# A transformer layer on one core: the last block product of an output projection made of seven smaller ones

## The chip, the cores and the metric

The kernel runs on one core of one Trainium2 chip. The time is the device time of one execution in microseconds; the number that counts is the median of the timed runs. The core has five engines: the PE (TensorE, matmuls; its weight loads are listed apart as PEld), DVE (VectorE), ACT (ScalarE), POOL (GpSimd), and SP (SyncE), which here only issues DMAs.

## The reference, cut to what matters

512 tokens, 2048 features, all in float32.

```
h = rmsnorm(x, norm_g)
y = attention(h)                      # 32 query heads, 4 key heads, window of 128, gated by silu
x = x + y @ w_out                     # "out projection", 512 x 2048 by 2048 x 2048
g = sigmoid(rmsnorm(x, ple_norm) @ ple_gate)
x = x + (p @ ple_proj) * g            # "gate stage"
return rmsnorm(x, final_g)
```

## The kernel before, in words

A product in float32 is made of three matmuls in a reduced format (`mm3`, lines 124 to 126): each operand is split into a high part (a cast by ACT) and a low part (operand minus high part, by DVE), and high x high, high x low and low x high are summed in PSUM.

The out projection and the gate stage each take a 512 x 2048 by 2048 x 2048 product as two by two blocks, made of seven block products instead of eight (Strassen's scheme in Winograd's form). The order of the seven is `ORDER_OUT = (1, 7, 2, 6, 5, 3, 4)`. Each product takes one sum of token blocks (a "form", made by `Forms.steps`, L734 to L747, in place in the tiles `gate`) and one sum of weight blocks. The sums of weights of products 7, 5 and 6 are made early, in DRAM, by copies and accumulating DMAs (`sum_weights`). Products 6 and 4 share one chain: the weights of product 6 are loaded into eight tiles `grown`, and as soon as they are split an accumulating DMA of POOL's queue adds another block to them for product 4 (L628).

Each product has two column halves (`jj`) and four pieces each. A piece is 256 rows by 512 columns of weights, 1024 columns in the tile; twelve matmuls of 512 columns use it. So the out projection has 56 pieces. `Pieces` (L613 on) looks after them: `_prepare` loads a piece into `braw` (three buffers) by a DMA of SP's queue, `_split` casts it into `bhi` (ACT, L641) and subtracts into `blo` (DVE, L642; three buffers each), and `ahead(i)` splits up to piece i + 2 and loads up to piece i + 3 when piece i is used.

Results are added to the residual tiles `x1` by `add_y` (DVE, L955 and L957), and `squares` (ACT, L924) sums their squares. `turn` transposes finished rows of `x1` (four transposes of 128 x 128 on the PE, L938) and writes them, times a gain, into `hT` (ACT, L941). These turns stand beside product 4 and the first product of the gate stage, whose forms (`fhg`, `flg`) come from `hT`.

In this part of the kernel only the PE and SP keep the written order. A scheduler places the instructions of DVE, ACT and POOL, and the program's data order then ties the engines by semaphores.

Of the kernel before, what the change touches and what calls it, by code (L numbers as in the profile page):

```python
# [11 lines left out]
F32 = mybir.dt.float32  # L12
# [43 lines left out]
def trunk_kernel(ctx: ExitStack, tc: tile.TileContext, a: dict):  # L56
# [557 lines left out]
    class Pieces:  # L614
# [2 lines left out]

        def __init__(self):
            self.specs, self.base, self.made, self.grown, self.due = [], {}, {}, {}, []

        def add(self, kind, srcs, key=None):
            self.specs.append((kind, srcs, key))
# [12 lines left out]
            self.base[i] = t  # L635

        def _split(self, i):
            raw = self.base.pop(i)
            hi = wpool.tile([P, WE], F32R, tag="whi", name=f"bhi{i}")
            lo = wpool.tile([P, WE], F32R, tag="wlo", name=f"blo{i}")  # L640
            nc.scalar.copy(hi, raw)  # L641
            nc.vector.tensor_sub(lo, raw, hi.bitcast(F32))  # L642
# [12 lines left out]
        def ahead(self, i):  # L655

            last = len(self.specs) - 9
            for n in range(max(i, 0), min(i + 6, last) + 1):
                kind = self.specs[n][0]
                if n not in self.base and n >= self.done and kind != "grow" and (kind == "seed" or n <= i + 3):  # L660
                    self._prepare(n)
            while self.done <= min(i + 2, last):
                self._split(self.done)
                self.done += 1

        def get(self, i):
            self.ahead(i)

            key = self.specs[i][2]
            if key is not None:  # L670
                n = next((n for n in range(i + 1, len(self.specs)) if self.specs[n][2] == key), None)
                if n is not None:
                    self.due.append((i + 6, n))
            while self.due and self.due[0][0] <= i:
                self._prepare(self.due.pop(0)[1])
            return self.made.pop(i)

    B = Pieces()

    def add_stage(nm, order):  # L680
        at = {}

        def add_embeds(p, jj):
            if nm == "ple_gate" and p in (1, 5, 3, 4):
                j = jj + 2 * (p in (5, 3))
                B.add("proj", a["ple_proj"].rearrange("(k p) d -> p k d", p=P)[:, :, j * 512 : (j + 1) * 512])

        for p in order:
            for jj in range(2):
                if nm == "ple_gate" and (p, jj) == (4, 0):  # L690
                    for v in range(2):
                        at["e", v] = len(B.specs)
                        add_embeds(p, v)
                at[p, jj] = len(B.specs)
                for m in range(4):
# [4 lines left out]
                    growing = (6, 4) if (nm, 6) in SUMS else (7, 6, 4)  # L700
# [6 lines left out]
    at_out = add_stage("w_out", ORDER_OUT)  # L707
    at_ple = add_stage("ple_gate", ORDER_PLE)

    class Forms:  # L710
# [6 lines left out]
        def steps(self, p):  # L717

            self.made[p] = []
            for h in range(2):  # L720
                a11, a21 = self.q[h][:, :, :256], self.q[h][:, :, 256:]
                a12, a22 = self.q[2 + h][:, :, :256], self.q[2 + h][:, :, 256:]
                if self.nm == "o":
                    src, sub = {
                        1: (a11, None), 7: (a11, (a21, a11)), 2: (a12, None), 6: (a11, (a22, a11)),
                        5: (a21, (a21, a22)), 3: (a12, (a12, a11)), 4: (a22, None),
                    }[p]
                else:
                    src, sub = {
                        2: (a12, None), 7: (a21, (a21, a11)), 1: (a11, None), 6: (a21, (a22, a21)),  # L730
                        5: (a11, (a11, a21)), 3: (a12, (a12, a21)), 4: (a22, None),
                    }[p]
                if sub:
                    nc.vector.tensor_sub(src, *sub)  # L734
# [135 lines left out]

    late = pool("late", reuse_waits="tile")
    rooms.append(late)
    x1 = [late.tile([P, NB, 512], F32, name=f"x1_{j}") for j in range(4)]
    fg = late.tile([P, D], F32, name="fg")
    pTh = late.tile([P, 2, S], F32R, name="pTh")
# [6 lines left out]
    def banks(p, jj, nm):  # L882

        if p in (6, 5, 3):
            return chain[jj]
        tag = ("to" if p in (7, 2) else "sp")[jj]
# [38 lines left out]

    hT = {}

    def turn(kp, th, tag):

        g = kp // 2  # L930
        if g not in hT:
            hT[g] = quarter(f"hT{g}")
        tp = bank(f"tp{kp}_{th}", tag)
        for n in range(2):
            k = 2 * kp + n
            for tb in range(2):
                src = x1[k // 4][:, 2 * th + tb, (k % 4) * P : (k % 4 + 1) * P]
                nc.tensor.transpose(tp[:, (2 * n + tb) * P : (2 * n + tb + 1) * P], src, ident)  # L938
        for n in range(2):
            k = 2 * kp + n  # L940
            nc.scalar.mul(hT[g][:, k % 4, th * 256 : th * 256 + 256], tp[:, n * 256 : n * 256 + 256], pn[:, k : k + 1])  # L941

    ple_forms = Forms(hT, "g")
    ple_first = ple_forms.steps(2)
# [15 lines left out]

    turns = []

    x_at = {(1, 1, 1): 0, (7, 0, 0): 2, (7, 0, 3): 1, (7, 1, 1): 3}
    waiting = {(7, 0): (1, 0), (2, 0): (1, 1)}
    held = {}
    for n, p in enumerate(ORDER_OUT):
        nxt = out_forms.steps(ORDER_OUT[n + 1]) if n < 6 else iter(())
        for jj in range(2):
            later.extend(held.pop(waiting.get((p, jj)), ()))
            calls = iter(range(4))  # L970

            def todo():
                part = x_at.get((p, jj, next(calls)))
                if part is not None:
                    load_x(part)
                next(nxt, None)
                if p == 4:
                    for tag in "to":
                        if turns:
                            turn(*turns.pop(0), tag)  # L980
                    if jj:
                        next(ple_first, None)

            ps = unit(p, jj, at_out, out_forms, todo)
            posts = [partial_of(add_y, p, jj, tb, ps[tb]) for tb in range(2)]
            if p == 1:
                held[p, jj] = posts
            else:
                later.extend(posts)
        run(nxt)  # L990
        if p == 6:
            nc.sync.dma_start(fg, a["final_g"].partition_broadcast(P))
        if p == 3:
            turns = [(kp, 0) for kp in range(8)] + [(kp, 1) for kp in range(4, 8)]
    run(ple_first)
    assert not turns

# [72 lines left out]

    spare = late.tile([P, 2 * WE], F32R, name="spare")
# [12 lines left out]
    for n, p in enumerate(ORDER_PLE[:-1]):  # L1086
        nxt = ple_forms.steps(ORDER_PLE[n + 1])
        for jj in range(2):
            calls = iter(range(4))

            def todo():
                k = early.get((p, jj, next(calls)))
                if turns:
                    turn(*turns.pop(0), "s")
# [184 lines left out]
```

## Time and profile before

| | before |
|---|---|
| median of 3 runs | 799.96 us (799.6 to 800.24) |
| the profiled execution | 798.73 us, span 797.0 us, granted clock 0.997 |
| PE busy | 785.5 us, 99% |
| DVE busy | 590.5 us, 74% |
| ACT busy | 482.7 us, 61% |
| POOL busy | 149.6 us, 19% |
| out projection on the PE | 452.52 to 610.28 us, 56 pieces |

All times inside the profile count from the start of its span. The span is what the profiler saw from the first to the last instruction; the execution's own time has a little around it. Busy matmul time is modelled and counts overlapping matmuls, so the distance between the starts of two matmuls says what one costs.

### The profile page before, as it was taken

To read this page: it belongs to the slowest core of one execution; us is meant where nothing else is said; L and a number is where in the kernel's file an instruction comes from. 1 tells how busy PE (TensorE), PEld (TensorE's weight loads), DVE (VectorE), ACT (ScalarE), POOL (GpSimd) and SP (SyncE) were. 2 spreads that over 40 slices of the span, in tenths; PEclk is the share of its full clock that TensorE was granted. 3 is DMA by queue.
4 is the path that set the end of the run, shared out by engine and by line. 5 is a ranking of instruction groups with operands and counts; after the bars stand their busy time and mean duration, and the time that the engine had idled before them with its cause. 6 is when DMAs were issued, how large, how long until landed. Compare 5 with 4: busy or idle time off the path is not lost.

```text
span 797.0 us, 11130 instructions
## 1 busy us (share of the span) xinstructions
PE 785.5 (99%) x3760; PEld 656.1 (82%) x3760; DVE 590.5 (74%) x1013; ACT 482.7 (61%) x992; POOL 149.6 (19%) x363
## 2 busy tenths in 40 slices
PE   9999999999999999999999999999999999999995
PEld 7888888888888888888888888888888888878884
DVE  4436478888877787787887898766656977979686
ACT  5632377677556766566665654555568756758545
POOL 0003013443243314332133200030000020200000
PEclk9999999999999999999999999999999999999998
DMA  8790586889687967879585578998503996885533
GB/s 336 279 212 11 187 237 180 235 211 260 175 226 193 220 199 211 213 207 260 155 220 135 151 267 312 353 258 249 197 26 118 358 208 211 163 212 194 176 106 106
DMA packets 44073, 163.99 MB, mean 206 GB/s; under 512 B 6304, under 2 KB 6944, under 8 KB 40176
## 3 DMA queue, kind: packets, MB, share of 16 engines
q1 hardware_dynamic: 36896, 129.01, 48.1%
q0 software_dynamic: 6832, 33.88, 23.0%
q8 instruction: 29, 0.48, 0.2%
q10 hardware_dynamic: 288, 0.39, 0.1%
q14 instruction: 28, 0.23, 0.1%
HBM read 157.44 MB, written 46.19 MB: 255 GB/s over the span
## 4 chain that ended last, share of the span: by engine, by line
PE 85%; issue 7%; DMA 3%; DVE 3%; POOL 1%; ACT 1%; SPq 0%; DVEq 0%; POOLq 0%; ACTq 0%
PE qps L126 7%; PE qps L124 7%; PE qps L125 7%; PE gps L124 7%; PE gps L125 7%; PE gps L126 7%; PE o L124 6%; PE o L126 6%; PE o L125 6%; PE s L401 2%; PE g L125 2%; PE g L126 2%; PE g L124 2%; PE o L523 2%; PE vps L228 2%
## 5 line engine op out<-in xcount | busy, mean ns | idle before, releaser
L642 DVE TENSOR_TENSOR blo<-braw,bhi 128x1024 fp32r<-128x1024 f32 x80 | 97.7, 1223 | 40.4 <-ACT bhi L641 40.2
L641 ACT CAST bhi<-braw 128x1024 fp32r<-128x1024 f32 x80 | 84.0, 1051 | 56.3 <-PE o L126 16.4
L124 PE MATMUL gps<-xh,whi 128*128 128x512 f32 x256 | 100.5, 393 | 0.0
L125 PE MATMUL gps<-xl,whi 128*128 128x512 f32 x256 | 100.0, 391 | 0.0
L126 PE MATMUL gps<-xh,wlo 128*128 128x512 f32 x256 | 99.9, 390 | 0.0
L503 POOL TENSOR_SCALAR_AFFINE_SELECT own<-r 64x256 fp32r<-64x256 f32 x96 | 61.2, 637 | 193.0 <-ACT r L484 109.3
L113 DVE TENSOR_TENSOR wlo<-wraw,whi 128x1024 fp32r<-128x1024 f32 x60 | 73.5, 1226 | 25.8 <-ACT whi L107 24.3
L124 PE MATMUL qps<-xh,whi 128*128 128x512 f32 x224 | 87.7, 392 | 0.0
L124 PE MATMUL o<-bhi,fho 128*128 128x512 f32 x224 | 87.7, 391 | 0.0
L125 PE MATMUL qps<-xl,whi 128*128 128x512 f32 x224 | 87.4, 390 | 0.0
L126 PE MATMUL qps<-xh,wlo 128*128 128x512 f32 x224 | 87.3, 390 | 0.0
L126 PE MATMUL o<-bhi,flo 128*128 128x512 f32 x224 | 87.2, 389 | 0.0
L125 PE MATMUL o<-blo,fho 128*128 128x512 f32 x224 | 87.2, 389 | 0.0
L461 ACT ACTIVATE t<-t,sm 128x129 f32<-128x129 f32 x128 | 50.6, 397 | 49.3 <-DVE sm L452 46.5
L125 PE MATMUL g<-blo,fhg 128*128 128x512 f32 x192 | 74.8, 390 | 0.4 <-DVE blo L642 0.4
L124 PE MATMUL g<-bhi,fhg 128*128 128x512 f32 x192 | 75.1, 391 | 0.0
L126 PE MATMUL g<-bhi,flg 128*128 128x512 f32 x192 | 74.8, 390 | 0.0
L107 ACT CAST whi<-wraw 128x1024 fp32r<-128x1024 f32 x60 | 62.1, 1037 | 16.1 <-DMA wraw<-in_w_q 16.1
L484 ACT CAST r<-pt 128x256 fp32r<-128x256 f32 x64 | 23.8, 372 | 55.4 <-PE pt L479 55.1
L126 PEld LDWEIGHTS gps<-xh,wlo 128*128 128x128 f32 x256 | 48.1, 188 | 10.6
L124 PEld LDWEIGHTS gps<-xh,whi 128*128 128x128 f32 x256 | 48.1, 188 | 9.1
L125 PEld LDWEIGHTS gps<-xl,whi 128*128 128x128 f32 x256 | 48.1, 188 | 8.7
(204 smaller groups left out, 1699.4 us busy)
## 6 DMA issues: line engine op xcount, KB each, us to landing
wraw<-in_w_gate_in SPq DMA_DIRECT2D x32, 512.0 KB, 5.4
wraw<-in_w_q SPq DMA_DIRECT2D x28, 512.0 KB, 6.2
w_out<-in_w_out POOLq DMA_DIRECT2D x24, 512.0 KB, 7.8
braw<-in_w_out SPq DMA_DIRECT2D x24, 512.0 KB, 4.0
braw<-in_ple_gate SPq DMA_DIRECT2D x24, 512.0 KB, 4.3
w_out<-in_w_out SPq DMA_DIRECT2D x16, 512.0 KB, 7.6
ple_gate<-in_ple_gate SPq DMA_DIRECT2D x16, 512.0 KB, 6.5
ple_gate<-in_ple_gate POOLq DMA_DIRECT2D x16, 512.0 KB, 6.1
```

The source lines that it names most:

```text
L107: nc.scalar.copy(hi, self.raw[i])
L113: nc.vector.tensor_sub(lo, raw, hi.bitcast(F32))
L124: nc.tensor.matmul(ps, sh, mh, start=first, stop=False, skip_group_check=more)
L125: nc.tensor.matmul(ps, sh, ml, start=False, stop=False, skip_group_check=more)
L126: nc.tensor.matmul(ps, sl, mh, start=False, stop=last, skip_group_check=more)
L228: nc.tensor.matmul(v_ps[t], h[:, c], both[:, :, 256:512], start=f, stop=e, skip_group_check=True)
L401: nc.tensor.matmul(s_ps[:, u, : 2 * n], st, key[:, :, first : first + n], start=True, stop=True)
L461: nc.scalar.activation(su, su, AF.Exp, bias=sm[:, u : u + 1], accum_out=sm[:, 2 + u : 3 + u])
L484: nc.scalar.copy(r[:, 0], PT[i])
L503: nc.gpsimd.affine_select(out=cols(own[places[g % 2 ^ low]]), in_=cols(r[here, low].bitcast(F32)), pattern=[[sign * QB, 2], [0, GROUP], [s ...
L641: nc.scalar.copy(hi, raw)
L642: nc.vector.tensor_sub(lo, raw, hi.bitcast(F32))
```

## The change

Product 4 of the out projection, 256 tokens by 1024 by 1024, is made of seven products of half the size by the same scheme, in the order `ORDER_IN = (1, 7, 6, 2, 5, 4, 3)`. Each has two weight pieces ("n" in the list below) of six matmuls. They are interleaved with the pieces of product 3, the sixth of the order. The out projection then has 62 pieces: 48 of twelve matmuls and 14 of six.

The token sums of the small products (`differences`: four subtractions of 512 columns) and the weight sums (`sums` and `split`: eight additions of 1024 columns) are GpSimd instructions. The accumulating DMAs go out four pieces behind the use of a piece of product 6, instead of six (`GROW`). From piece 8 to piece 87 every fourth split goes to a fourth place, the tile `spare`, and splits and loads run one piece further ahead. Of the sixteen turns' evacuations into `hT`, six go to DVE. The turns stand between the pieces, and use other PSUM banks. Two subtractions move from DVE to GpSimd: that of `pTl`, and one half of a form of the gate stage.

```diff
 def _split(self, i):
-    raw = self.base.pop(i)
-    hi = wpool.tile([P, WE], F32R, tag="whi", name=f"bhi{i}")
-    lo = wpool.tile([P, WE], F32R, tag="wlo", name=f"blo{i}")
+    kind, whose, key = self.specs[i]
+    raw = whose.raw(*key) if kind == "part" else self.base.pop(i)
+    if self.first4 <= i < self.last4 and i % 4 == 3:
+        hi, lo = rooms[1][:, :WE], rooms[1][:, WE:]
+    else:
+        hi = wpool.tile([P, WE], F32R, tag="whi", name=f"bhi{i}")
+        lo = wpool.tile([P, WE], F32R, tag="wlo", name=f"blo{i}")
     nc.scalar.copy(hi, raw)
-    nc.vector.tensor_sub(lo, raw, hi.bitcast(F32))
+    (nc.gpsimd if i in self.aside else nc.vector).tensor_sub(lo, raw, hi.bitcast(F32))
...
+    if kind == "part":
+        whose.split(*key)
...
-    while self.done <= min(i + 2, last):
+    while self.done <= min(i + (3 if self.first4 <= i < self.last4 - 2 else 2), last):
...
+GROW = 4
+FOURTH = 8, 90
+ORDER_IN = (1, 7, 6, 2, 5, 4, 3)
+class Inside:
+    def grow(self, key):
+        nm, jj, m = key
+        nc.gpsimd.dma_start(B.grown[key], block(nm, 2, 1, jj, m), accum_op=ALU.add)
...
+    def sums(self):
+        for i in range(2):
+            nc.gpsimd.tensor_add(self.s7[:, i], self.t[0, 1, i], self.t[1, 1, i])
+            yield
+            nc.gpsimd.tensor_add(self.t[0, 1, i], self.t[0, 1, i], self.t[0, 0, i])
+            yield
...
+    def split(self, q, i):
+        b11 = self.t[0, 0, i]
+        if q == 1:
+            nc.gpsimd.tensor_add(b11, b11, self.s7[:, i])
+        elif q == 7:
+            nc.gpsimd.tensor_add(self.s7[:, i], b11, self.t[1, 0, i])
+    def differences(self):
...
+        for out, x, y in (f[0], v(1, 0), v(0, 0)), (f[1], v(1, 1), f[0]), (f[2], v(1, 0), v(1, 1)), (f[3], v(0, 1), f[1]):
+            nc.gpsimd.tensor_sub(out, x, y)
+            yield
...
+SHARED = [(3, 0, 0), (3, 0, 1), "n", (3, 0, 2), "n", "n", (3, 0, 3), "n", (3, 1, 0), "n", "n", (3, 1, 1), "n", "n", (3, 1, 2), (3, 1, 3)]
+SHARED += ["n"] * (14 - SHARED.count("n"))
+OUT = [(p, jj, m) for p in (1, 7, 2, 6, 5) for jj in range(2) for m in range(4)] + SHARED
...
-                    nc.vector.tensor_sub(src, *sub)
+                    (nc.gpsimd if (self.nm, p, h) == ("g", 7, 0) else nc.vector).tensor_sub(src, *sub)
...
+VECTOR_TURNS = {(0, 0), (2, 0), (4, 1), (5, 1), (6, 1), (7, 1)}
...
+def inner_part():
+    x = None
+    for q in ORDER_IN:
...
+        for i in range(2):
+            bh, bl = B.get(at)
+            fh, fl = inside.made[q]
+            for kk in range(2):
+                k = 2 * i + kk
+                mm3(ps, fh[:, k], fl[:, k], bh[kk], bl[kk], q in (1, 7, 2, 4) and k == 0, k == 3, q in (6, 5, 3))
...
+extra = {
+    (5, 0, 0): [differences], (5, 0, 1): [differences], (5, 0, 2): [differences], (5, 0, 3): [differences],
+    (5, 1, 1): [inner_forms, inside.begin, inner_sums], (5, 1, 2): [inner_forms, inner_sums],
+    (5, 1, 3): [inner_forms, inner_sums], (3, 0, 0): [inner_forms, inner_sums],
+    (3, 0, 1): [partial_of(turn, 0, 0, "o")],
...
-nc.vector.tensor_sub(pTl, pT, pTh.bitcast(F32))
+nc.gpsimd.tensor_sub(pTl, pT, pTh.bitcast(F32))
```

In the changed kernel the splits stand on L646 (ACT) and L647 (DVE), the differences on L737, the sums of weights on L712, L714, L725 and L727, and the inner products' adds to `x1` on L1114 and L1116.

More of the change, by code (lines that the diff above doesn't have):

```diff
@@ L659, in ahead @@
                 kind = self.specs[n][0]
-                if n not in self.base and n >= self.done and kind != "grow" and (kind == "seed" or n <= i + 3):
+                if n not in self.base and n >= self.done and kind not in ("grow", "part") and (kind == "seed" or n <= i + (4 if self.first4 <= i < self.last4 - 2 else 3)):
                     self._prepare(n)
-            while self.done <= min(i + 2, last):
+            while self.done <= min(i + (3 if self.first4 <= i < self.last4 - 2 else 2), last):
                 self._split(self.done)
@@ L667, in get @@
             self.ahead(i)
-            key = self.specs[i][2]
-            if key is not None:
+            kind, _, key = self.specs[i]
+            if kind in ("seed", "grow"):
                 n = next((n for n in range(i + 1, len(self.specs)) if self.specs[n][2] == key), None)
                 if n is not None:
-                    self.due.append((i + 6, n))
+                    self.due.append((i + 6, partial_of(self._prepare, n)))
+                elif key[0] == inside.nm:
+                    self.due.append((i + GROW, partial_of(inside.grow, key)))
@@ L680, in add_stage @@
+    inside = Inside("w_out")
+    SHARED = [(3, 0, 0), (3, 0, 1), "n", (3, 0, 2), "n", "n", (3, 0, 3), "n", (3, 1, 0), "n", "n", (3, 1, 1), "n", "n", (3, 1, 2), (3, 1, 3)]
+    SHARED += ["n"] * (14 - SHARED.count("n"))
+    OUT = [(p, jj, m) for p in (1, 7, 2, 6, 5) for jj in range(2) for m in range(4)] + SHARED
     def add_stage(nm, order):
         at = {}
+        if nm == inside.nm:
+            parts = [(q, i) for q in ORDER_IN for i in range(2)]
+            for step in OUT:
+                if step == "n":
+                    B.add("part", inside, parts.pop(0))
+                    continue
+                p, jj, m = step
+                if (nm, p) in SUMS:
+                    src = summed[nm, p, jj, m]
+                else:
+                    src = block(nm, *{1: (1, 1), 2: (2, 1), 3: (2, 2), 6: (1, 1)}[p], jj, m)
+                B.add("seed" if p == 6 else "one", src, (nm, jj, m) if p == 6 else None)
+            return
@@ L872, in trunk_kernel @@
     rooms.append(late)
+    spare = late.tile([P, 2 * WE], F32R, name="spare")
+    rooms.append(spare)
+    B.first4, B.last4 = FOURTH
     x1 = [late.tile([P, NB, 512], F32, name=f"x1_{j}") for j in range(4)]
@@ L940, in turn @@
             k = 2 * kp + n
-            nc.scalar.mul(hT[g][:, k % 4, th * 256 : th * 256 + 256], tp[:, n * 256 : n * 256 + 256], pn[:, k : k + 1])
+            out, src = hT[g][:, k % 4, th * 256 : th * 256 + 256], tp[:, n * 256 : n * 256 + 256]
+            if (kp, th) in VECTOR_TURNS:
+                nc.vector.tensor_scalar_mul(out, src, pn[:, k : k + 1])
+            else:
+                nc.scalar.mul(out, src, pn[:, k : k + 1])
     ple_forms = Forms(hT, "g")
@@ L961, in trunk_kernel, with part @@
     turns = []
+    def part(p, jj):
+        ps = banks(p, jj, "o")
+        f = out_forms.made[p]
+        first = p not in (6, 5, 3)
+        for m in range(4):
+            fh, fl = f[m]
+            bh, bl = B.get(at)
+            for kk in range(2):
+                k = 2 * m + kk
+                for tb in range(2):
+                    mm3(ps[tb], fh[:, kk, blk(tb)], fl[:, kk, blk(tb)], bh[kk], bl[kk], first and k == 0, k == 7, not first)
+            if m == 3:
+                posts = [partial_of(add_y, p, jj, tb, ps[tb]) for tb in range(2)]
+                if p == 1:
+                    held[p, jj] = posts
+                else:
+                    coming.extend(posts)
+            yield
@@ new lines, in inner_part @@
+    def inner_part():
+        x = None
+        for q in ORDER_IN:
+            if q in (1, 7, 2, 4):
+                ps = bank(f"o4_{q}", {1: "t", 4: "t"}.get(q, "o"))
+                x = ps if q == 1 else x
+            else:
+                ps = x
+            for i in range(2):
+                bh, bl = B.get(at)
+                fh, fl = inside.made[q]
+                for kk in range(2):
+                    k = 2 * i + kk
+                    mm3(ps, fh[:, k], fl[:, k], bh[kk], bl[kk], q in (1, 7, 2, 4) and k == 0, k == 3, q in (6, 5, 3))
+                if i == 1:
+                    coming.append(partial_of(add_in, q, ps))
+                yield
@@ new lines, in add_in @@
+    def add_in(q, ps):
+        whither = {
+            1: [((0, 0), -1)], 2: [((0, 0), 1)], 7: [((1, 1), 1), ((1, 0), -1)], 6: [((1, 0), -1)],
+            5: [((1, 1), 1)], 3: [((0, 1), 1)], 4: [((1, 0), 1)],
+        }[q]
+        for (r, c), sign in whither:
+            j, t = c, 2 + r
+            xt = x1[j][:, t, :]
+            if sign > 0:
+                nc.vector.tensor_add(xt, ps, xt)
+            else:
+                nc.vector.tensor_sub(xt, xt, ps)
+            if q in (2, 5, 3, 4):
+                squares(t, j)
@@ L963, in trunk_kernel, with turns_of @@
+    def turns_of(*v):
+        for kp, th, tag in v:
+            turn(kp, th, tag)
     x_at = {(1, 1, 1): 0, (7, 0, 0): 2, (7, 0, 3): 1, (7, 1, 1): 3}
     waiting = {(7, 0): (1, 0), (2, 0): (1, 1)}
[L965 to L991, printed above, removed]
+    held, coming = {}, []
@@ new lines, in trunk_kernel @@
+    inner_sums, differences, inner_forms = inside.sums(), inside.differences(), inside.forms()
+    extra = {
[3 more added lines that the diff above has]
+        (3, 0, 1): [partial_of(turn, 0, 0, "o")],
+        (3, 0, 3): [partial_of(turn, 1, 0, "o")],
+        (3, 1, 0): [partial_of(turn, 2, 0, "o")],
+        (3, 1, 1): [inner_forms, partial_of(turn, 3, 0, "o")], (3, 1, 2): [inner_forms], (3, 1, 3): [inner_forms],
+        7: [partial_of(turn, 4, 0, "s")], 8: [partial_of(turn, 5, 0, "s"), ple_first],
+        9: [partial_of(turn, 4, 1, "o"), ple_first], 10: [partial_of(turn, 6, 0, "p"), partial_of(turn, 7, 0, "p")],
+        11: [partial_of(turn, 5, 1, "o"), ple_first],
+        12: [partial_of(turn, 6, 1, "o"), ple_first], 13: [partial_of(turn, 7, 1, "o")],
+    }
@@ new lines, in trunk_kernel @@
+    made, inner, seen = {}, inner_part(), 0
+    ahead = {p: out_forms.steps(n) for p, n in zip((1, 7, 2, 6, 5), (7, 2, 6, 5, 3))}
+    for at, step in enumerate(OUT):
+        if step == "n":
+            next(inner)
+            step, p = seen, None
+            seen += 1
+        else:
+            p, jj, m = step
+            if m == 0:
+                made[p, jj] = part(p, jj)
+                later.extend(held.pop(waiting.get((p, jj)), ()))
+            next(made[p, jj], None)
+        for _ in range(-(-len(later) // 2)):
+            later.pop(0)()
+        later.extend(coming)
+        coming.clear()
+        if step in x_at:
+            load_x(x_at[step])
+        if p in ahead:
+            next(ahead[p], None)
+            if (jj, m) == (1, 3):
+                run(ahead[p])
+        for f in extra.get(step, ()):
+            next(f, None) if hasattr(f, "send") else f()
+        if step == (6, 1, 3):
@@ L992, in trunk_kernel @@
             nc.sync.dma_start(fg, a["final_g"].partition_broadcast(P))
-        if p == 3:
-            turns = [(kp, 0) for kp in range(8)] + [(kp, 1) for kp in range(4, 8)]
+    turns = []
     run(ple_first)
@@ L1069, in gate_later @@
         later[:0] = [partial_of(run, z) for z in gate(*v)]
-    spare = late.tile([P, 2 * WE], F32R, name="spare")
     rooms4 = {}
@@ L1093, in todo @@
                 if turns:
-                    turn(*turns.pop(0), "s")
+                    turn(*turns.pop(0), "t")
                     if not turns:
```

38 lines of the change are left out of this document (34 added, 4 removed).

## The prediction

> **What bounds the kernel now.** I read the page first, then what the PE waits for, then the windows and timelines of the out projection.
>
> ```profile
> span 797.0 us, 11130 instructions
> PE 785.5 (99%) x3760; PEld 656.1 (82%) x3760; DVE 590.5 (74%) x1013; ACT 482.7 (61%) x992; POOL 149.6 (19%) x363
> PE 85%; issue 7%; DMA 3%; DVE 3%; POOL 1%; ACT 1%; SPq 0%; DVEq 0%; POOLq 0%; ACTq 0%
> ...
> PE g L125 <- DVE blo L642: 0.4, 1, 0.4
> ...
> 460.00:480.00 20.00, 20.00 (x90) 16.53 (x90) 19.74 (x23) 9.48 (x11) 0.00 (x0) 1.00 0.85 301
> 540.00:560.00 20.00, 20.00 (x89) 16.54 (x89) 13.17 (x15) 11.13 (x16) 0.00 (x0) 1.00 0.76 241
> ```
>
> The PE is busy throughout (second line), holds 85% of the chain (third), and waits 0.4 us for a weight split (fourth). In the window rows the columns are PE, PEld, DVE, ACT and POOL busy time, the granted clock, the DMA share and GB/s. From 460 to 480 the DVE too is full, 19.74 of 20 us; from 540 to 560 it has 6.8 us free. So time falls only if the PE issues less, and any delay of the DVE near 460 may reach the PE.
>
> **The saving on the PE.** A product of four 1024-column pieces and two column halves is 96 matmuls of 512 columns. Product 4 becomes seven products of 4 x 3 = 12, 84 in all: twelve fewer. The compiled order agrees, 3544 rows against 3556. The 390 ns of a matmul is not its price, since they overlap:
>
> ```profile
> 455.29 0.39 PE L124 MATMUL o<-bhi,fho 128*128 128x512 f32 x1
> ...
> 458.01 0.39 PE L124 MATMUL o<-bhi,fho 128*128 128x512 f32 x1
> ...
> 590.29 0.48 PE L124 MATMUL o<-bhi,fho 128*128 128x512 f32 x1
> ...
> 593.90 0.48 PE L124 MATMUL o<-bhi,fho 128*128 128x512 f32 x1
> ```
>
> A piece of twelve matmuls starts 2.72 us after the piece before it, so one costs 0.227 us and twelve 2.72 us. With two turns (eight transposes) between, a piece takes 3.61 us, so a turn costs 0.44 us. Twelve turns stay in the out projection, singly or in pairs, and single ones cost no more per turn: 0. **Saving 2.72 us.**
>
> **GpSimd's operations and the VectorE.** New on GpSimd are four differences of 512 columns, eight sums of 1024 columns, and two subtractions of 1024 moved from DVE. GpSimd is idle then, so their own time costs nothing; what they hold back on the DVE may.
>
> ```profile
> 442.44 1.29 POOL L503 TENSOR_SCALAR_AFFINE_SELECT own<-r 64x256 fp32r<-64x256 f32 x1 [2.53 <-ACT r L484]
> ...
> 450.81 1.43 POOL L503 TENSOR_SCALAR_AFFINE_SELECT own<-r 64x256 fp32r<-64x256 f32 x1 [2.65 <-DVE r L492]
> ...
> 442.14 1.23 DVE L642 TENSOR_TENSOR blo<-braw,bhi 128x1024 fp32r<-128x1024 f32 x1 [1.64 <-ACT bhi L641]
> 443.28 1.49 DVE L113 TENSOR_TENSOR wlo<-wraw,whi 128x1024 fp32r<-128x1024 f32 x1
> ...
> L113 DVE TENSOR_TENSOR wlo<-wraw,whi x60: 1203/1224/1491, 59.7 to 443.3; 128x1024 fp32r<-128x1024 f32 x60
> ...
> L503 POOL TENSOR_SCALAR_AFFINE_SELECT own<-r x96: 497/504/1595, 126.2 to 450.8; 64x256 fp32r<-64x256 f32 x96
> ...
> L354 POOL TENSOR_TENSOR diffs<-values x2: 732/741/750, 75.9 to 77.5; 64x256 f32<-64x256 f32 x2
> ```
>
> The select of 442.44 lasts 1.29 us instead of its median 0.504: it sits until the DVE's split ends at 443.37. The DVE's next subtraction, of two SBUF operands, then lasts 1.491 instead of 1.224. So the two engines take turns, GpSimd gets in between two DVE instructions that stand back to back, and a select of 0.504 holds the DVE for 0.27, its length less 0.23. A two-operand GpSimd instruction on 256 columns lasts 0.735 to 0.74, so by the same 0.23 it holds 0.50. I take twice that for 512 columns, **1.0 us**, and **2.0** for 1024. The lower end is the select's own 0.27 whatever the size; the upper is the whole duration, 1.47 and 2.94. I lean to 1.0 because that end shares the operand count and the measured hold.
>
> [...]
>
> **Where the four differences land.** They are written beside product 5, but only PE and SP keep written order here; in the compiled order they stand first on GpSimd, ahead of the eight accumulating loads. The first waits only for the last attention matmul (about 452.2), the others for the fourth gate product of L561 (459.5).
>
> ```profile
> 451.71 0.40 PE L523 MATMUL o<-r,V 128*128 128x256 f32 x2
> ...
> 450.67 2.62 DVE L734 TENSOR_TENSOR gate<-gate 128x1024 f32<-128x1024 f32 x2
> 453.21 0.68 DVE L570 TENSOR_TENSOR gate<-gps,rb 128x512 f32<-128x512 f32 x1
> 453.81 1.21 DVE L642 TENSOR_TENSOR blo<-braw,bhi 128x1024 fp32r<-128x1024 f32 x1
> ...
> 457.03 2.49 DVE L561 SCALAR_TENSOR_TENSOR gate<-gate,u 128x512 f32<-128x512 f32 x4
> 459.44 2.35 DVE L642 TENSOR_TENSOR blo<-braw,bhi 128x1024 fp32r<-128x1024 f32 x2
> ...
> 465.79 1.22 DVE L642 TENSOR_TENSOR blo<-braw,bhi 128x1024 fp32r<-128x1024 f32 x1
> ...
> 469.11 0.39 PE L125 MATMUL o<-blo,fho 128*128 128x512 f32 x1
> ...
> 701.51 1.22 DVE L642 TENSOR_TENSOR blo<-grown,bhi 128x1024 fp32r<-128x1024 f32 x1
> ...
> 702.78 0.50 PE L125 MATMUL g<-blo,fhg 128*128 128x512 f32 x1 [0.41 <-DVE blo L642]
> ```
>
> The first gets in at 453.29, when L734 ends, and holds to 454.29. L570 reads PSUM and passes; the split of piece 2, due at 453.81, moves by 0.48. The other three each come between DVE instructions behind 459.5 (splits 3, 4, a form, split 5), 1.0 each. Nothing on the DVE is idle until then, so split 6, at 465.79, is 0.48 + 3.0 = 3.48 late. It ends at 467.01 in the trace, and the PE reads it at 469.11; a split reaches the PE 0.05 after its end (702.73 to 702.78). The cover is 2.10 - 0.05 = 2.05 us, and **1.43 us** reach the PE. Splits 8 and 10 have more cover. From piece 11 on the fourth place lets a split start up to one piece, 2.72 us, earlier, which covers what comes later.
>
> **The interleaved end.** Of its 22 pieces 14 have six matmuls, 1.36 us, and each still wants a full cast and split:
>
> ```profile
> L642 DVE TENSOR_TENSOR blo<-braw,bhi 128x1024 fp32r<-128x1024 f32 x80 | 97.7, 1223 | 40.4 <-ACT bhi L641 40.2
> L641 ACT CAST bhi<-braw 128x1024 fp32r<-128x1024 f32 x80 | 84.0, 1051 | 56.3 <-PE o L126 16.4
> ...
> 506.68 1.28 DVE L955 TENSOR_TENSOR x<-o,x 128x512 f32<-128x512 f32 x2
> ...
> 73.79 0.47 DVE L311 TENSOR_SCALAR values<-vps,rstd 128x256 f32<-128x256 f32 x1
> ```
>
> Added are six splits (14 pieces for 8), 6 x 1.22 on DVE and 6 x 1.05 on ACT, four adds of 0.6 (two take 1.28, overlapping), and twelve turn evacuations that go from ACT to DVE (0.4 each by L311, the nearest PSUM row). I followed the DVE's compiled order on the old clock: pieces 40 to 48 start at 561.4, 564.1, 567.3, 568.6, 571.3, 572.7, 574.1, 577.2 and 578.6. The tightest place is where GpSimd makes product 4's weights out of product 7's. Split 45 ends about 570.2; then 46 to 571.3, a sum (2.0) to 573.3, split 47 to 574.5, a sum to 576.6 (beside an add that reads PSUM), split 48 to 577.8. The PE wants 48 at 578.8: 1.0 us to spare, stall **0**. Without that cover every further microsecond is paid in full. Later splits (51, 52, 53) keep about 1 us by the same count. The first four sums run between 535 and 550, where the DVE has free time and the fourth place gives about 5 us: 0, where four holds in a row without any free time would be 8 us, 3 late.
>
> SP's loads are the old ones, and only each split frees a raw buffer, so they move with the splits. The PSUM banks of the turns wait for the add of product 7, due at about 584, before the fourth turn at 587.2. The two subtractions moved to GpSimd fall in the gate stage: 1.22 off the DVE, up to 2.0 held, with the fourth place as cover: 0.
>
> **A stall that may shrink.** The 0.56 us at 702.2 to 702.8 stands behind casts that wait for accumulating loads:
>
> ```profile
> 694.94 1.06 ACT L649 CAST last<-grown 128x1024 fp32r<-128x1024 f32 x1 [1.46 <-DMA grown<-in_ple_gate]
> ```
>
> Three of these eight loads can start a piece earlier, because the fourth place lasts to piece 87; the rest cannot. Between 0 and 0.56 I take half, **0.28 us** gained.
>
> **Sum.** -2.72 + 1.43 + 0 - 0.28 = -1.57 us. The profiled execution took 798.73, its span 797.0 with 1.73 around it; its span becomes 795.4. The median of the runs, 799.96, is 1.23 above that execution; the same step gives **798.4 us**.
>
> **Rivals.** First, *the cover holds*: the differences hold no more than a select, 4 x 0.27 = 1.08, under 2.05, so nothing reaches the PE: 799.96 - 2.72 - 0.28 = 797.0. For it: 0.27 is the only hold measured. Against: a two-operand instruction lasts 0.23 longer at the same size.
>
> Second, *GpSimd holds the DVE for its whole duration*, and it ends slower. With 1.47 the first difference delays 0.95 and the others 4.41; less 2.05, 3.31 reach the PE. With 2.94 the four sums between 561 and 580 push split 48 to 581.4, 2.6 late. -2.72 + 3.31 + 2.6 - 0.28 = +2.9: 802.9. Holding between, the stall is 1.43 plus 4 us, and beyond the 1.0 us of spare another 7.6, per unit of excess over my holds: 22% more wins nothing, and from 36% more (1.36 us for 512 columns) the kernel is slower by 1.6. For it: back-to-back GpSimd rows show no gap to prove that the hold ends early with two operands. Against: 0.27 of 0.50.
>
> Third, *the change doesn't do what it says*, the interleaving not hiding the splits: the fewer matmuls are certain, so that is only a smaller version of the second.
>
> **Chances.** Forecast 0.47 (797.7 to 799.2, by holds 20% either way), first rival 0.28, second 0.20, something unseen 0.05. A measurement of this kernel can tell 0.2%, 1.6 us, that is below 798.36 or above 801.56. Faster: 0.28 and half of the forecast's, less a little, 0.49; slower: 0.20 and 0.02, 0.22; the same: 0.29. The range 796.8 to 801.2 takes in both likelier cases and the milder part of the second rival.
>
> **What would show it.** In the new profile: PE waits for the split of L647 between 460 and 470, about 1.4 us in all; four GpSimd rows L737 there, one before 455 and three behind 459, and DVE splits of about 2.2 us beside them; no such wait from 560 to 610; 84 matmuls for the inner products; the wait near 700 halved. Wrong would be: no wait near 460 (first rival), or waits at 575 to 590 (second).

## The result, and the profile after

The changed kernel takes **804.7 us** (median of 6 runs, 803.99 to 805.71) against 799.93 for the kernel before: a ratio of **1.0060**, 95% interval 1.0047 to 1.0072. It is slower, by about 4.8 us, where 1.6 us less was forecast. The profiled execution took 805.71 us with a span of 804.0, against 797.0 before: 7.0 us to find. (That execution is 1.0 above the median of its kernel, and the one before 1.2 below; so the profiles lie further apart than the medians.)

The page of the changed kernel (busy times, then the chain of waits), and what TensorE waits for:

```profile
span 804.0 us, 11152 instructions
PE 787.7 (98%) x3748; PEld 654.9 (81%) x3748; DVE 617.4 (77%) x1036; ACT 485.3 (60%) x989; POOL 183.8 (23%) x377
PE 76%; issue 9%; DVE 7%; DMA 3%; ACT 2%; POOL 1%; DVEq 0%; POOLq 0%; ACTq 0%
...
PE o L125 <- DVE blo L647: 4.0, 4, 1.7
PE g L125 <- DVE blo L647: 1.3, 2, 0.8
```

TensorE has its twelve matmuls less (3748 for 3760), but its busy time rose, 785.5 to 787.7, and the waits for splits of weights rose from 0.4 to 5.3 us. DVE's part of the chain went from 3% to 7%. The windows say in which stretches (PE, PEld, DVE, ACT, POOL, granted clock, DMA share, GB/s; the last two rows are for TensorE alone: PE, clock, DMA share, GB/s):

```profile
460.00:480.00 20.00, 19.00 (x82) 14.73 (x81) 20.00 (x20) 9.08 (x11) 6.06 (x3) 1.00 0.62 215
540.00:560.00 20.00, 18.25 (x73) 14.37 (x72) 11.79 (x11) 6.38 (x7) 10.37 (x4) 0.91 0.76 243
560.00:580.00 20.00, 20.00 (x92) 16.53 (x91) 18.45 (x18) 14.03 (x22) 6.32 (x3) 1.00 0.47 149
580.00:600.00 20.00, 18.55 (x90) 15.03 (x89) 20.00 (x21) 13.68 (x22) 4.15 (x2) 1.00 0.31 99
...
552.00:556.00 4.00, 2.25 (x9) 0.96 0.19 57
556.00:560.00 4.00, 4.00 (x13) 0.61 0.55 170
```

From 556 to 560 TensorE is busy throughout, and yet does 13 matmuls where 18 fit: its clock is at 0.61. TensorE's timeline there and at the next wait:

```profile
552.76 0.50 PE L124 MATMUL o<-bhi,fho 128*128 128x512 f32 x1
554.98 0.50 PE L125 MATMUL o<-blo,fho 128*128 128x512 f32 x1 [1.71 <-DVE blo L647]
...
555.85 0.63 PE L125 MATMUL o<-blo,fho 128*128 128x512 f32 x1
556.27 0.63 PE L126 MATMUL o<-bhi,flo 128*128 128x512 f32 x1
...
584.66 0.40 PE L124 MATMUL o<-bhi,fho 128*128 128x512 f32 x1
586.50 0.50 PE L125 MATMUL o<-blo,fho 128*128 128x512 f32 x1 [1.45 <-DVE blo L647]
```

After a start-to-start gap of 2.22 us, seven matmuls follow at 0.42 to 0.43 instead of 0.227 and one at 0.36, about 1.6 us more. From 552.34 to 559.19 stand 13 matmuls, 2.95 us by that price, so the place costs **3.9 us** in all. I measure every place so, by what the starts lie apart beyond 0.227. (The expectations of the runs below count 4.1 for it, and 5.8 together with the wait at 584; that is 0.2 too much.)

From the first out-projection matmul to the first of the gate stage took 157.76 us before and 162.82 after, +5.06: 2.72 saved, 1.80 lost at 460 to 471, **3.9** at 552 to 559, **1.72** at 584, 0.4 in small pieces. In the gate stage the old stall of 0.67 near 702 became two, 0.81 at 699 and 1.41 at 708: +1.55. Those, 0.14 from an attention end that came later and 0.2 that I didn't place make up the 7.0.

**At 460 to 471** the trace is the one predicted. DVE and GpSimd (POOL):

```profile
460.08 3.44 DVE L647 TENSOR_TENSOR blo<-braw,bhi 128x1024 fp32r<-128x1024 f32 x2
463.45 1.77 DVE L841 TENSOR_TENSOR flo<-gate,fho 128x512 fp32r<-128x512 f32 x1
465.15 2.31 DVE L647 TENSOR_TENSOR blo<-braw,bhi 128x1024 fp32r<-128x1024 f32 x1
...
452.46 2.11 POOL L737 TENSOR_TENSOR inner<-gate 128x512 f32<-128x512 f32 x1
460.24 2.20 POOL L737 TENSOR_TENSOR inner<-gate,gate 128x512 f32<-128x512 f32 x1 [5.67 <-DVE gate L561]
462.41 3.97 POOL L737 TENSOR_TENSOR inner<-gate,inner 128x512 f32<-128x512 f32 x2
```

One difference before 455, three behind 459, and beside each of these a DVE instruction that is 1.08 us too long: 3.44 for two splits of 2.35, 1.77 for a form of 0.69, 2.31 for a split of 1.22.

**At 545 to 590** the same thing happens with the sums of weights, 1024 columns each:

```profile
552.74 6.63 DVE L647 TENSOR_TENSOR blo<-braw,bhi 128x1024 fp32r<-128x1024 f32 x3 [6.04 <-ACT bhi L646]
568.60 2.51 DVE L752 TENSOR_TENSOR il<-gate,ih 128x512 fp32r<-128x512 f32 x1
575.43 2.92 DVE L647 TENSOR_TENSOR blo<-sum,bhi 128x1024 fp32r<-128x1024 f32 x1
579.41 3.43 DVE L647 TENSOR_TENSOR spare<-sum,spare 128x1024 fp32r<-128x1024 f32 x1
583.36 3.09 DVE L647 TENSOR_TENSOR blo<-braw,bhi 128x1024 fp32r<-128x1024 f32 x1
...
546.63 2.39 POOL L712 TENSOR_TENSOR sum<-grown,grown 128x1024 f32<-128x1024 f32 x1 [12.15 <-DMA grown<-in_w_out]
551.45 2.39 POOL L712 TENSOR_TENSOR sum<-grown,grown 128x1024 f32<-128x1024 f32 x1
553.92 3.23 POOL L714 TENSOR_TENSOR grown<-grown,grown 128x1024 f32<-128x1024 f32 x1
568.16 2.40 POOL L725 TENSOR_TENSOR grown<-grown,sum 128x1024 f32<-128x1024 f32 x1 [11.01 <-DVE blo L647]
...
544.39 1.05 ACT L646 CAST spare<-braw 128x1024 fp32r<-128x1024 f32 x1 [2.10 <-DMA braw<-w_out]
551.66 1.05 ACT L646 CAST bhi<-braw 128x1024 fp32r<-128x1024 f32 x1 [6.22 <-DMA braw<-w_out]
```

The form at 568.60 is 1.82 us too long, the three splits behind it 1.70, 2.22 and 1.88: a sum holds DVE for 1.9 us on average. But there is a second suspect at 552. The scalar engine (ACT) waited 6.22 us for the load of piece 36, so DVE stood idle until 552.74, while TensorE had used up the lead. The two suspects are theory **F** (late loads) and theory **H** (the holds alone), and the experiments began there.

F had a cause to offer, in SP's timeline. The final gains (`fg`, 1 MB) were issued at 513.52 before. Now they come at 536.73, since the fourth place puts one more weight load, which must wait for a split, ahead of them; the loads of pieces 36 to 39 follow at once:

```profile
512.66 24.02 SPq L635 DMA_DIRECT2D braw<-w_out  x4
536.73 0.48 SPq L1167 DMA_DIRECT2D fg<-in_final_g  x1
539.08 16.19 SPq L635 DMA_DIRECT2D braw<-w_out  x4
```

### The profile page after: what moved, and what is told of

Its sections match the earlier page's. It is cut to its first block, busy times and chain, and to the rows that moved or that the text cites. A ratio compares the mean times of both kernels' runs of the same rounds, so it can differ in the third digit from the quotient of the medians.

```text
span 804.0 us, 11152 instructions
## 1 busy us (share of the span) xinstructions
PE 787.7 (98%) x3748; PEld 654.9 (81%) x3748; DVE 617.4 (77%) x1036; ACT 485.3 (60%) x989; POOL 183.8 (23%) x377
## 4 chain that ended last, share of the span: by engine, by line
PE 76%; issue 9%; DVE 7%; DMA 3%; ACT 2%; POOL 1%; DVEq 0%; POOLq 0%; ACTq 0%
PE qps L124 7%; PE qps L126 7%; PE qps L125 7%; PE gps L124 7%; PE gps L125 7%; PE gps L126 7%; PE o L125 4%; PE o L124 4%; PE o L126 4%; DVE blo L647 3%; PE s L401 2%; PE g L125 2%; PE g L126 2%; PE g L124 2%; PE vps L228 2%
## 5 line engine op out<-in xcount | busy, mean ns | idle before, releaser
L647 DVE TENSOR_TENSOR blo<-braw,bhi 128x1024 fp32r<-128x1024 f32 x66 | 87.9, 1336 | 32.1 <-ACT bhi L646 32.0
L646 ACT CAST bhi<-braw 128x1024 fp32r<-128x1024 f32 x66 | 69.3, 1050 | 50.8 <-DMA braw<-w_out 12.2
L113 DVE TENSOR_TENSOR wlo<-wraw,whi 128x1024 fp32r<-128x1024 f32 x60 | 73.4, 1225 | 27.4 <-ACT whi L107 26.0
L125 PE MATMUL g<-blo,fhg 128*128 128x512 f32 x168 | 65.6, 391 | 1.3 <-DVE blo L647 1.3
L124 PE MATMUL g<-bhi,fhg 128*128 128x512 f32 x168 | 65.9, 392 | 0.1
L126 PE MATMUL g<-bhi,flg 128*128 128x512 f32 x168 | 65.5, 390 | 0.0
L125 PE MATMUL o<-blo,fho 128*128 128x512 f32 x148 | 58.9, 398 | 4.2 <-DVE blo L647 4.0
L124 PE MATMUL o<-bhi,fho 128*128 128x512 f32 x148 | 58.5, 395 | 0.0
L126 PE MATMUL o<-bhi,flo 128*128 128x512 f32 x148 | 58.3, 394 | 0.0
```

The lines of the kernel that those rows point to most:

```text
L124: nc.tensor.matmul(ps, sh, mh, start=first, stop=False, skip_group_check=more)
L125: nc.tensor.matmul(ps, sh, ml, start=False, stop=False, skip_group_check=more)
L126: nc.tensor.matmul(ps, sl, mh, start=False, stop=last, skip_group_check=more)
L647: (nc.gpsimd if i in self.aside else nc.vector).tensor_sub(lo, raw, hi.bitcast(F32))
```

## The experiments

Each ratio is to executions of the kernel before that were taken along with the run: their median is 799.58 us for runs 1 to 4, 799.38 for 5 to 8 and 799.09 for 9 and 10. The changed kernel's 1.0060 is to its own 799.93.

**1. The gains earlier again.**

```diff
-        if step == (6, 1, 3):
+        if step == (6, 1, 2):
             nc.sync.dma_start(fg, a["final_g"].partition_broadcast(P))
```

> The changed kernel with the load of the final gains (1 MB) issued one piece earlier in SP's order, so that it stands ahead of the weight load of piece 35 again, as it did before the change. Theory F (late loads): the fourth place put that weight load, which waits for a split, ahead of the gains; their 1 MB then ran from 536.7 to 550 beside the loads of pieces 36 to 39. F expects the gains to be issued near 513, the scalar engine to wait less than 3 us for weights between 540 and 556, the wait at 552 and the half-speed stretch behind it (together 4.1 us) to go, and some of the 1.7 at 584 with them: 804.7 becomes 799 to 800.6. Theory H (the four sums hold VectorE, 2.2 us each, and that alone makes the wait at 552): the wait at 552 stays at 1.5 us or more, 803.5 to 804.7.

Measured: 805.6 us, ratio 1.0071 (1.0056 to 1.0086). Not faster at all. The gains were issued at 516.18, piece 36 was cast at 549.17 instead of 551.66, and the wait at 552 went. TensorE's timeline shows where the time went instead:

```profile
575.61 0.39 PE L124 MATMUL o<-bhi,ih 128*128 128x512 f32 x1
577.07 0.50 PE L125 MATMUL o<-blo,ih 128*128 128x512 f32 x1 [1.07 <-DVE blo L647]
...
582.93 0.40 PE L124 MATMUL o<-bhi,fho 128*128 128x512 f32 x1
585.15 0.50 PE L125 MATMUL o<-blo,fho 128*128 128x512 f32 x1 [1.83 <-DVE blo L647]
```

0.49 at 561, 1.23 at 575.61, and 1.99 at 582.93 with the half-speed stretch now behind that one. The gate stage began at 615.71, against 615.48 in the changed kernel. So the late load decided *where* TensorE waited, not how long. Both theories as I had put them fall: F, since time did not change; H, since the wait at 552 went. A third, **T**, takes their place: DVE has too little time between 546 and 590 for its own work and the holds, and a shortage removed at one place comes back at the next.

**2. The differences later.** DVE first writes two elements of their room from product 2's result, so GpSimd has to wait for that.

```diff
+            nc.vector.tensor_copy(room[:, ::2, 0, 0:1], x1[0][:, 0, 0:2].rearrange("p (a b) -> p a b", b=1))
             for out, x, y in (f[0], v(1, 0), v(0, 0)), ...
                 nc.gpsimd.tensor_sub(out, x, y)
```

> The changed kernel with the four differences of GpSimd made to wait for the end of product 2 (two elements of their room are written by VectorE from product 2's result first). Theory F and H alike: VectorE's splits at 460 to 466 lose their 1.08 us holds and the three waits of 460 to 471 (1.8 us together) go; the holds fall at 515 to 522, where VectorE has room. 804.7 becomes 802.9; the stalls at 552 and 584 stay. A rival, that the waits of 460 to 471 come from something else than the differences, expects no change there; if the moved differences delay the accumulating loads, the wait at 552 grows instead by up to 3 us.

Measured: 801.68 us, ratio 1.0037 (1.0023 to 1.0051). TensorE waits nowhere from 452 to 551; the differences ran from 511 to 518, and the splits at 460 to 466 have their normal lengths again:

```profile
460.31 2.35 DVE L647 TENSOR_TENSOR blo<-braw,bhi 128x1024 fp32r<-128x1024 f32 x2
...
511.12 1.29 POOL L738 TENSOR_TENSOR inner<-gate 128x512 f32<-128x512 f32 x1 [58.00 <-DVE inner L736]
```

By the ratios 1.8 us are gained, as expected (3.0 by the medians). Its runs lie in two groups, 800.8 to 801.7 and 803.6 to 804.6; the profiled one is of the upper, and has a wait of 2.03 us at 581.24 with a half-speed stretch behind it. That the lower group lacks that stretch is likely, but not shown: its granted clocks are 0.996 and 0.997 in four of five runs, with 0.993 in the fifth, and 0.993 to 0.995 in the upper group.

**3. The kernel before, with its gains late.** Only the place of that load changes.

```diff
+                if step == (5, 0, 0):
+                    nc.sync.dma_start(fg, a["final_g"].partition_broadcast(P))
...
-        if p == 6:
-            nc.sync.dma_start(fg, a["final_g"].partition_broadcast(P))
```

> The kernel before, with nothing changed but the load of the final gains, which is issued one weight load later, as the changed kernel has it. F expects the same late weights: the gains issued at about 535, the scalar engine waiting for the loads of pieces 36 to 38 until 551, and, as there is no fourth place here, a wait of 3 to 5 us on TensorE near 550: 799.9 becomes 803 to 805. H expects no change, 799.9.

Measured: 799.12 us, ratio 0.9999 (0.9987 to 1.0011): nothing. The gains were issued at 536.87, and piece 36 was cast at 547.90 instead of 547.08. F's premise, that late gains alone make these loads so late, is gone from this side too. Why piece 36 was cast only at 551.66 in the changed kernel stays open, beyond the 2.5 us that run 1 took off.

**4. No fourth place.**

```diff
-    FOURTH = 8, 90
+    FOURTH = 8, 8
```

> The changed kernel without the fourth place for split weights, in the out projection and in the gate stage. F: SP's order is the old one, so the gains load early and the loads of pieces 36 to 39 come in time, but each split has 2.7 us less lead: the wait at 552 is 0 to 3 us, the one at 584 1.7 to 4.4 us, and the waits at 699 and 708 (0.8 and 1.4) become the one of 0.67 that the kernel before had. 802 to 805. H: less lead makes every hold dearer, the wait at 552 grows beyond 4 us: 806 or more.

Measured: 804.16 us, ratio 1.0060 (1.0043 to 1.0077), the same as with it. The three waits of 460 to 471 are as before; behind them the out projection's waits come in seven pieces (4.1 us together, the longest 1.13 at 549.10, no half speed), and the two stalls of the gate stage are one of 1.40. H's 806 is off. The time lies in F's range, which doesn't tell F from T, since T had made no forecast for this run. The fourth place, which the prediction counted on as cover, is worth nothing in the sum.

**5. The sums left out.** The eight additions are dropped, and products 7 and 4 take one unsummed block each; this computes something else.

```diff
-                nc.gpsimd.tensor_add(self.s7[:, i], self.t[0, 1, i], self.t[1, 1, i])
-                nc.gpsimd.tensor_add(self.t[0, 1, i], self.t[0, 1, i], self.t[0, 0, i])
...
-                nc.gpsimd.tensor_add(b11, b11, self.s7[:, i])
-                nc.gpsimd.tensor_add(self.s7[:, i], b11, self.t[1, 0, i])
```

> The changed kernel with the eight sums of GpSimd left out (product 7's and 4's weights are then one block each, and products 1, 5, 6, 2 and 3 read blocks that nothing was added to): the output is another, the matmuls, casts, splits and loads are as many as before. Theory T (VectorE's time between 546 and 590 is full, because eight sums hold it 1.7 to 2.2 us each; the waits at 552 and 584 are two places at which the same shortage shows, and a shortage removed at one place comes back at the other): both go, 5.8 us, and 804.7 becomes 799 to 799.5, with the waits of 460 to 471 and of 699 to 708 left. A rival, F (late loads), expects the wait at 552 to stay at 1.5 us or more with the loads as late as they were: 801 or more.

Measured: 800.25 us, ratio 1.0011 (1.0000 to 1.0021), the profiled execution 799.82. TensorE waits nowhere between 471 and 690. So the sums cost 3.9 us by the ratios, and the whole of the waits at 552 and 584 in the profile. The median is 0.75 above what T said.

**6. The sums on VectorE**, behind product 5's first adds, by the same means as in 2.

```diff
+            nc.vector.tensor_copy(s7[:, :, 0, 0:1], x1[2][:, 2, 0:2].rearrange("p (a b) -> p a b", b=1))
...
-                nc.gpsimd.tensor_add(self.s7[:, i], self.t[0, 1, i], self.t[1, 1, i])
+                nc.vector.tensor_add(self.s7[:, i], self.t[0, 1, i], self.t[1, 1, i])
```

(and the other three in the same way)

> The changed kernel with the eight sums on VectorE instead of GpSimd, the first of them behind product 5's first adds (two elements of the room are written from their result, so that VectorE does not wait for the accumulating loads). Each costs VectorE about 1.14 us (a 1024-column subtraction issued back to back) instead of a hold of 1.7 to 2.2. T: VectorE gets back 5 to 8 us between 546 and 590 and the waits at 552 and 584 shrink to under 1 us together: 799 to 800.5. A rival (VectorE is full either way, a sum costs it as much as a hold) expects 803 to 805.

Measured: 802.18 us, ratio 1.0033 (1.0023 to 1.0042). Its profiled execution, the fastest of its runs (801.01), has one wait of 0.96 us between 471 and 690 where the changed kernel has 5.6. The direction is T's, the size is short: 2.2 us by the ratios, where 4.2 to 5.7 were expected. The median run is 1.2 us slower than the profiled one, and no trace shows where it lost them.

**7. The fourth place for the out projection only.**

```diff
-    FOURTH = 8, 90
+    FOURTH = 8, 64
```

> The changed kernel with the fourth place for split weights given up at piece 64, early in the gate stage, instead of piece 90. If the end of the fourth place is what reorders the casts before the last accumulating loads, the two waits near 699 and 708 (0.81 and 1.41 us) become one of 0.6 to 1.0, as the kernel before has it: 803.3 to 803.9. If the gate stage's waits come from its later start or from GpSimd's two subtractions, they stay: 804.7.

Measured: 803.64 us, ratio 1.0053 (1.0038 to 1.0068). The gate stage has one wait again, 0.83 at 706.93. So the end of the fourth place makes the second stall, which cost 1.1 us by the medians and 0.6 by the ratios; the intervals overlap, so only the profile settles it. The time alone couldn't, since the edit also moved the out projection's waits (0.31 at 553, 0.48 at 556, 2.05 at 582; 162.01 us from its first matmul to the gate stage's, instead of 162.82).

**8. All of 1, 2, 6 and 7.**

> The changed kernel with the differences of GpSimd behind product 2, the sums on VectorE behind product 5's first adds, the fourth place up to piece 64 only, and the final gains loaded one piece earlier. T: 1.8 us from the differences, 5 to 5.8 from the sums, about 1.2 from the gate stage, so the twelve matmuls (2.72) are nearly all gained: 796.5 to 798.5, faster than either kernel. If VectorE is full with the sums on it, 801 or more.

Measured: **797.81 us** (10 runs, 797.42 to 798.82), ratio **0.9977** (0.9968 to 0.9986): faster than both kernels. Its waits and windows (in the second part DVE is the third figure):

```profile
span 796.1 us, 11148 instructions
...
PE g L125 <- DVE blo L647: 0.8, 1, 0.8
PE o L125 <- DVE blo L647: 0.5, 1, 0.5
...
560.00:575.00 15.00, 14.48 (x66) 11.64 (x66) 15.00 (x17) 8.54 (x14) 0.00 (x0) 1.00 0.33 106
575.00:590.00 15.00, 15.00 (x73) 12.38 (x72) 15.00 (x18) 10.72 (x18) 0.00 (x0) 1.00 0.32 105
```

The out projection takes 156.03 us, 1.73 less than before; what of the 2.72 is missing is a wait of 0.67 at 572.5, and small pieces. DVE is busy for the whole 30 us from 560 to 590, with nothing to spare, but it keeps up.

**9. The same with the sums back on GpSimd.**

> The kernel of the run with all three edits, but with the eight sums back on GpSimd: differences behind product 2, fourth place up to piece 64, final gains one piece earlier. T: the eight holds of about 1.9 us take 4 to 6 us from TensorE wherever the lead runs out, between 550 and 590: 801.5 to 803.5. A rival, the prediction's own step (the holds fit, with 1.0 us to spare at split 48, once nothing before them is late): no wait over 0.7 us between 540 and 600, 797.5 to 799.

Measured: 802.14 us, ratio 1.0038 (1.0024 to 1.0051). The waits are 0.39 and 0.48 near 555, 1.31 at 573.97 and 2.03 at 581.32. This is the prediction's own step put by itself, with nothing late before it, and the holds do not fit: piece 36 is cast at 546.98, as in the kernel before (547.08). Nor were GpSimd's results late as such: between 540 and 600 no cast, split or matmul waits for GpSimd in this trace, and every wait of TensorE is for a split by DVE. DVE's timeline:

```profile
548.06 8.95 DVE L647 TENSOR_TENSOR blo<-braw,bhi 128x1024 fp32r<-128x1024 f32 x3 [3.54 <-ACT bhi L646]
565.70 2.51 DVE L753 TENSOR_TENSOR il<-gate,ih 128x512 fp32r<-128x512 f32 x1
572.53 2.92 DVE L647 TENSOR_TENSOR blo<-sum,bhi 128x1024 fp32r<-128x1024 f32 x1
576.51 3.42 DVE L647 TENSOR_TENSOR spare<-sum,spare 128x1024 fp32r<-128x1024 f32 x1
580.45 3.08 DVE L647 TENSOR_TENSOR blo<-braw,bhi 128x1024 fp32r<-128x1024 f32 x1
```

Against normal lengths (three splits back to back about 3.5, a form 0.69, a split 1.22) this is 5.45 + 1.82 + 1.70 + 2.20 + 1.86 = 13.0 us of holds. The same eight sums on DVE take 8 x 1.14 = 9.1, by their distance to the next instruction in run 8, as here:

```profile
554.14 1.23 DVE L713 TENSOR_TENSOR sum<-grown,grown 128x1024 f32<-128x1024 f32 x1
555.29 1.22 DVE L647 TENSOR_TENSOR spare<-braw,spare 128x1024 fp32r<-128x1024 f32 x1
```

The 3.9 us between them are near the 4.1 by which the out projection is longer in run 9's trace than in run 8's (160.16 against 156.03). The times differ by 4.3 by the medians and 4.9 by the ratios.

**10. One turn's evacuations from DVE to the scalar engine**, in the kernel of run 8, to shorten DVE ahead of the wait that is left.

```diff
-    VECTOR_TURNS = {(0, 0), (2, 0), (4, 1), (5, 1), (6, 1), (7, 1)}
+    VECTOR_TURNS = {(2, 0), (4, 1), (5, 1), (6, 1), (7, 1)}
```

> The kernel of the run with all three edits, with the first turn's two evacuations on the scalar engine instead of VectorE, which is full from 560 to 590 in that run (0.87 us of VectorE just ahead of the split that TensorE waits for at 572.5). T: that wait of 0.67 us goes, 797.8 becomes 797.1; if the scalar engine's cast becomes the late one, no change, 797.8.

Measured: 798.31 us, ratio 0.9987 (0.9977 to 0.9997), not better than run 8. The wait at 572.4 stayed (0.58), and another of 0.90 came behind it at 574.5: the compiled order now has a sum (L728) ahead of the split that TensorE needs. Neither answer I had written is the right one.

## Why the prediction was wrong

The step that failed is the overlap of the eight sums of weights with DVE's own work: it was put at a stall of 0, and the sums cost 3.9 us when they are compared with none (run 5), and 4.9 when they are compared with the same sums on DVE and nothing else is late (run 9 against run 8), both by the ratios and each to about 1.3 us. In the profile the span is 8.6 us over the 795.4 that was forecast: 5.6 from the waits at 552 and 584, 1.8 from the gate stage's stall, 0.4 from the differences, and the rest in small pieces.

**The saving: right.** With most stalls gone, run 8 shows 1.73 of the 2.72 us, and its wait of 0.67 most of the rest. Twelve turns cost 5.34 us in the changed kernel and 5.29 for the old way; 0 was right too.

**The holds: right.** 1.0 us was taken for 512 columns and 1.08 is measured; 2.0 for 1024, and 1.9 is measured. Alone such instructions last 1.29 (at 511.12 in run 2) and 2.39 (at 546.63 in the changed kernel), so a hold is some 80% of GpSimd's duration. The slower rival, with holds of 1.47 and 2.94, came nearest to the time (802.9), and a wait did stand at 584, inside the 575 to 590 that was named as its sign. But its reason, the length of the holds, isn't so, and it had no wait at 552; that it came near is in part luck. The longer instructions beside the differences and the last four sums have both inputs in SBUF (1.77 for a form of 0.69 at 463.45, 2.92 for a split of 1.22 at 575.43); L570, which takes one input from PSUM, keeps its 0.68 us at 453.35, beside the first difference.

**The differences: right in mechanism, a little small.** 1.43 us was forecast and 1.80 measured, and run 2 took it away.

**The first four sums: the step that failed.** "The first four sums run between 535 and 550, where the DVE has free time and the fourth place gives about 5 us: 0". They ran from 546.6 to 557, since the accumulating loads landed only then (GpSimd waited 12.15 us for them); that is where splits 36 to 38 stand, and DVE's free time from 546.7 to 552.7 went by without work, as it waited for a late load. The place cost 3.9 us.

**The later sums: the same error.** "1.0 us to spare, stall **0**" at split 48. Split 45 was to end at 570.2; in run 9, with the differences out of the way, it ended at 575.5. Only 1.3 us of that are TensorE's own delay: piece 45 began at 573.97 instead of 572.7, and then waited for this split. I had followed DVE's order from a start on time, checked each place against its own cover, and counted the fourth place's lead at each of them anew. A lead is there once. Run 1 shows the consequence: with the wait at 552 removed, the same time was lost at 575 and 583. The sum to make was DVE's over the whole stretch. The row that sums up DVE's three windows from 546 to 590 in run 8 (length, busy time):

```profile
sum 44.00, DVE 40.81; mean DVE 13.60
```

Of the 40.8 us the sums are 9.1, so DVE's other work is 31.7. With 13.0 us of holds in place of the sums that makes 44.7 of 44 us, before any idle time for a load, and even in run 8 DVE was idle for 3.2 of the 44.

**Loads that move with the splits: wrong, and without cost.** The final gains went behind a load that waits for a split; runs 1 and 3 show no price beyond the noise.

**The stall near 700: wrong sign.** It was to shrink by 0.28, and grew by 1.55. Three accumulating loads did start earlier, 68.3, 70.5 and 73.4 us behind the stage's first matmul instead of 70.3, 73.3 and 75.6, but the fourth came at 81.3 instead of 79.2: when the fourth place ends, one split falls a step behind the cast of a last piece, which waits for such a load in the scalar engine's order. Run 7, which ends it sooner, has the old stall back; the sequence itself I read off the timelines only. The two subtractions moved to GpSimd cost nothing, as forecast: no wait stands between 616 and 690.

**The clock: not foreseen.** Behind the wait of 1.99 us at 552.76, with the granted clock at 0.61 from 556 to 560, eight matmuls took another 1.6 us.

## What to carry to other kernels

Work given to GpSimd wasn't free for VectorE here: an add of 1024 columns on GpSimd took 1.9 us from VectorE in the changed kernel, and 1.14 when VectorE did it itself in run 8. Count an engine's free time over the whole stretch in which its work is due, holds included, not slack place by place, for a lead that one wait has used isn't there for the next. And when an edit removes a wait but not the time, look for where the wait went before taking the cause as refuted or found.

## What the runs showed of the hardware

The half-speed stretch stands behind waits of about 2 us in these runs, not always. Four of the five such waits have it (1.99 in the changed kernel and in run 1, 2.03 in run 2, 2.05 in run 7); the 2.03 us of run 9 have not, and of the shorter ones, up to 1.61 us, none has. TensorE's windows of run 2 and of run 9 (PE, clock, DMA share, GB/s) behind a wait of the same length:

```profile
584.00:588.00 4.00, 4.00 (x14) 0.62 0.37 131
```

```profile
584.00:588.00 4.00, 4.00 (x21) 1.00 0.40 131
```

The stretch lasts 3.3 us in the changed kernel and 3.5 in run 2, eight matmuls. Why the waits of runs 2 and 9, both of 2.03 us, differ in this, no run shows.
